# A hybrid decoder layer on one core: four adaLN chunks weighted on VectorE, low halves and three products on GpSimd, and a new order of issue up to the fourth FFN slice

## The chip, the core and the metric

The kernel runs on one NeuronCore of a Trainium2 chip. The metric is the device time of one execution in microseconds (us). Five engines take part: TensorE (PE, its weight loads are shown apart as PEld), VectorE (DVE), ScalarE (ACT), GpSimd (POOL) and SyncE (SP), whose queue issues nearly all transfers. A difference of 0.2% is about what a measurement of this kernel can tell from no change; the prediction says where it uses that.

## The reference, cut to what matters

One decoder layer over 256 tokens of width 1024, in float32:

```python
mod = (c @ w_ada[l] + b_ada[l])[:, None, :]
sh1, sc1, g1, sh2, sc2, g2 = jnp.split(mod, N_MOD, axis=-1)
h = rmsnorm(x, norm1_g[l]) * (1.0 + sc1) + sh1
z = h @ w_in[l]                       # q | k | v | x-branch | gate-branch, 512 columns each
attn = moba_attention(rmsnorm(q), rmsnorm(k), v)      # 256 keys: one block, causal
xr = causal_dwconv(xr, lru_conv_w[l], lru_conv_b[l])
lru = rg_lru(xr, ...) * jax.nn.gelu(gr)
mix = jnp.concatenate([rmsnorm(lru, lru_out_g[l]), rmsnorm(attn, attn_out_g[l])], axis=-1)
x = x + g1 * (mix @ w_out[l])
h2 = rmsnorm(x, norm2_g[l]) * (1.0 + sc2) + sh2
up = causal_dwconv(h2 @ w_up[l], ffn_conv_w[l], ffn_conv_b[l])
gate, val = jnp.split(up, 2, axis=-1)
x = x + g2 * ((jax.nn.silu(gate) * val) @ w_down[l])
```

Inside `rg_lru`: r and i are sigmoids of two block-diagonal products, a = exp(-8 r softplus(-lambda)), u = sqrt(1 - a*a) * (i * x), and h(t) = a(t) h(t-1) + u(t).

## The kernel before, in words

Activations lie with the width on the partitions: 8 blocks (kt = 0 to 7) of 128 rows by 256 tokens. Weights stream from HBM once, 1 MB at a time, into a ring of six buffers `w`; the list `order` fixes the order of the loads, and `send` issues the next one when `used` has counted the last reader of a buffer. A 2048-column buffer is read in two parts of 1024 columns.

Each large product runs as three one-pass products of float32r halves: `hi` casts a part of `w` to its high half `wh` (ACT, or DVE where its last argument is 1), `lo` subtracts it to leave the low half `wl` (line 172), and the activations are split the same way (`h_hi`, `h_lo`, `mix_h`, `mix_l`, `gated_h`, `gated_l`). All matmuls are issued on line 65. The stages are:

- lin: q, k, x-branch and gate-branch (`lin(kt, out, i)`, i is which of the three products). Beside it DVE makes shift and scale of norm 1 per block from the `ada1` loads (`ada`, line 365), and `normed`, `h_hi`, `h_lo`.
- the LRU: `conv_a`, `conv_d` (line 423), `gate`, `sigm`, `decay_a`, `decay_t`, `root` (ACT), `one_more` (line 452), the three products `igx` (439), `recur_u` (455), `recur_g` (462), and the scans (458).
- attention: sums and inverse roots for q and k (`k_sum`, `qk_r`), then for each of 8 heads `s_max` (DVE), `s_exp` (ACT, line 670), transposes `p_T` (676), copies `p_copy`, and `pv`. The matmuls of v fill in.
- `wo(c, kt)`, the output projection, and `res`, which adds it to x times g1; then norm 2 (`res_sq`, `res_add`, `res_sum`, `norm_s`, `norm_r`, `norm_mm`).
- 22 FFN slices: `up(f, kt)`, `gated_*`, `down(f, m)`.

The vectors g1 (load chunks 2 to 5) and sc2 (chunks 6 to 9) are sums over the 1024 entries of c; `g1_mm` runs each chunk as 8 float32 matmuls in four row groups of TensorE, with c as weights (`ccol`), `g1_row` copies four chunks to SBUF, and `g1_col` turns them to columns.

Up to the middle of slice 3 the order on all engines is one hand-held list of calls; from there a loop issues the slices. Each engine runs its instructions in the order of that list, and waits where an input is not there yet. GpSimd has only constants to set up before the first weights arrive.

Of the kernel before, what the change touches and what calls it, by code (L numbers as in the profile page):

```python
# [13 lines left out]
P = 128  # L14
# [54 lines left out]
def hybrid_layer(ctx: ExitStack, tc: tile.TileContext, x_d, c_d, pk_d, bd_d, ada1_d, lin_d, v_d,  # L69
# [47 lines left out]
    def send(q=None):  # L117

        if len(sent) < len(order):
# [3 lines left out]
            uses[key] = {"g1": 2 if key[1] < 2 else 1, "ada1": 2, "s2": 2, "g2": 2}.get(key[0], 4)  # L123
# [314 lines left out]
    def igx():  # L438
        nc.vector.tensor_mul(lru("ig"), lru("ig"), lru("xc"))
# [14 lines left out]
    def recur_u():  # L454
        nc.vector.tensor_mul(lru("ig"), lru("ig"), lru("r"))
# [5 lines left out]
    def recur_g():  # L461
        nc.vector.tensor_mul(lru("gel"), lru("gel"), lru("xc"))
# [162 lines left out]
    def g1_row(g, e=0):  # L625
        T["row", g] = pp.tile([P, 256], F32, tag="row", name="row")
        affine(e, T["row", g], B["g1", g].t[:, 0:256])

    def g1_col(g):
        b = B["g1", g]  # L630
        b.reopen(2)
        for m in range(2):
            b.mm(b.t[:, 256 + 4 * m:260 + 4 * m], T["row", g][:, m * P:(m + 1) * P], sel4)

    def g1_add(g):
        s = B["g1", g].t[:, 256:264].rearrange("p (m j) -> p j m", m=2)
# [102 lines left out]
    def res_add(kt):  # L739
        nc.vector.tensor_add(T["s2", kt], T["s2", kt], T["s2", kt - 1])  # L740
# [142 lines left out]
    sp(6)
    lin(1, "q", 1)
    normed(0, 2)
    lin(1, "g", 0)
    lin(1, "q", 2)
    lin(1, "x", 0)
    h_hi(0, 2)
    lin(1, "g", 2)  # L890
    lin(2, "q", 0)
    lin(2, "k", 0)
    lo("lin", 2, 0)
    hi("lin", 3, 0)
    lo("lin", 2, 1)
    lin(2, "k", 2)
    lin(2, "x", 2)
    hi("lin", 3, 1)
    ada("ada1", 1, 0)
    lin(2, "x", 0)  # L900
    ada("ada1", 1, 1)
    lin(2, "q", 2)
    lin(2, "g", 2)
# [84 lines left out]
    table(AF.Exp)
    lin(6, "g", 0)
    ada("ada1", 5, 1)  # L990
    table(AF.Gelu_apprx_tanh)
    ada_add("ada1", 5)
    sp(11)
    normed(0, 7)
    lin(5, "k", 2)
    hi("lin", 7, 0)
    lin(6, "q", 0)
    sp(12)
    lin(6, "x", 0)
    lin(4, "q", 1)  # L1000
    lin(6, "q", 1)
    h_hi(0, 7, 1)
    lin(6, "g", 2)
    sp(13)
    hi("lin", 7, 1)
    lin(6, "g", 1)
    h_lo(0, 7)
    lin(6, "x", 2)
    lin(6, "k", 0)
    bd_copy(1)  # L1010
    lo("lin", 7, 0)
    lo("lin", 6, 1)
    lin(6, "x", 1)
    lin(7, "x", 1)
    lin(7, "x", 2)
    lin(7, "x", 0)
# [60 lines left out]
    sigm(0, 3)
    v(0, 0, 0)
    qk_r(6)
    g1_mm(2)  # L1080
    sp(17)
    qk_r(7)
    lo("v", 1, 0)
    qk_r(8)
    sp(16)
    sigm(0, 1)
    qk_r(9)
# [472 lines left out]
```

## Time and profile before

| | |
|---|---|
| median of 3 runs | 332.96 us (332.39 to 333.06) |
| the profiled execution | 332.59 us |
| its span, first to last instruction | 330.8 us |
| TensorE busy | 320.2 us, 97% of the span |
| VectorE busy | 263.0 us, 79% |
| ScalarE busy | 194.5 us, 59% |
| GpSimd busy | 4.6 us, 1% |
| granted TensorE clock, mean | 0.991 |

Shares are means over stages with different limits, and a matmul counts as busy until its modelled end, so TensorE's 97% does not say that it has no room. Weight-load time (PEld) and the number of matmuls in a stretch tell more.

### The profile page before, as it was taken

How to read it: one execution, taken by the hardware profiler on the slowest of the kernel's cores; microseconds unless marked ns; L12 is line 12 of the kernel's file. 1: busy time of each engine (PE TensorE's matmuls, PEld its weight loads, DVE VectorE, ACT ScalarE, POOL GpSimd, SP SyncE). 2: the span in 40 equal slices, each digit the busy share in tenths (PEclk: the TensorE clock that was granted, in tenths of full speed). 3: DMA queues.
4: the chain of work that ended last, by engine and by line, in shares of the span. 5: the costliest groups of instructions: out<-in, count | busy, mean ns of one | idle time of the engine just before them, and what ended most of it. 6: DMA issues, size and time to landing. Idle time of an engine off the chain costs nothing.

```text
span 330.8 us, 6467 instructions
## 1 busy us (share of the span) xinstructions
PE 320.2 (97%) x2608; PEld 302.6 (91%) x2608; DVE 263.0 (79%) x507; ACT 194.5 (59%) x328; POOL 4.6 (1%) x22
## 2 busy tenths in 40 slices
PE   7899999999999999899999999999999999999994
PEld 7789999767599996899999999999999999999994
DVE  2469999899999998968696788888888677685654
ACT  5635458999988245865566455464646464655520
POOL 5000000000000000000000000000000000000000
PEclk9999999999999999799999999999999999999998
DMA  7999999939355998836566557575849463300003
GB/s 224 337 405 408 410 408 422 411 136 385 131 162 206 345 407 316 348 129 254 167 223 248 174 214 264 206 293 183 323 146 364 135 242 133 129 0 2 3 0 127
DMA packets 18013, 77.89 MB, mean 235 GB/s; under 512 B 1600, under 2 KB 6336, under 8 KB 10944
## 3 DMA queue, kind: packets, MB, share of 16 engines
q1 hardware_dynamic: 17840, 77.34, 62.6%
q8 instruction: 20, 0.33, 0.4%
q10 hardware_dynamic: 144, 0.15, 0.2%
q14 instruction: 9, 0.07, 0.1%
HBM read 76.43 MB, written 1.05 MB: 234 GB/s over the span
## 4 chain that ended last, share of the span: by engine, by line
PE 69%; DVE 16%; ACT 6%; issue 3%; SPq 2%; DMA 2%; DVEq 0%; ACTq 0%
PE bank L65 68%; DVE wl L172 4%; DVE w L365 4%; DMA w<-in_dram 2%; DVE m L423 2%; ACT wh L144 1%; SPq L132 1%; DVE m L766 1%; PE bank L676 1%; DVE ht L381 1%; ACT p L670 1%; DVE m L794 1%; DVE m L458 1%; DVE wh L150 1%; SPq L181 1%
## 5 line engine op out<-in xcount | busy, mean ns | idle before, releaser
L172 DVE TENSOR_TENSOR wl<-w,wh 128x1024 fp32r<-128x1024 f32 x94 | 113.2, 1220 | 19.8 <-ACT wh L144 19.1
L144 ACT CAST wh<-w 128x1024 fp32r<-128x1024 f32 x90 | 92.1, 1043 | 43.6 <-PE bank L65 34.9
L65 PE MATMUL bank<-hh__1575,wh 128*128 128x256 f32 x352 | 71.6, 285 | 1.1 <-ACT hh__1575 L148 1.1
L65 PE MATMUL bank<-hl__1576,wh 128*128 128x256 f32 x352 | 71.7, 286 | 0.0
L65 PE MATMUL bank<-hh__1575,wl 128*128 128x256 f32 x352 | 71.6, 285 | 0.0
L65 PEld LDWEIGHTS bank<-hh__1575,wh 128*128 128x128 f32 x352 | 55.3, 193 | 1.3 <-ACT hh__1575 L148 1.3
L65 PEld LDWEIGHTS bank<-hl__1576,wh 128*128 128x128 f32 x352 | 55.6, 194 | 0.2 <-DVE hl__1576 L392 0.2
L65 PEld LDWEIGHTS bank<-hh__1575,wl 128*128 128x128 f32 x352 | 55.4, 194 | 0.2 <-DVE wl L172 0.2
L766 DVE SCALAR_TENSOR_TENSOR m<-bank,pk,m 128x255 f32<-128x255 f32 x88 | 40.4, 479 | 19.0 <-ACT m L758 17.4
L65 PE MATMUL bank<-pl,wh 128*128 128x256 f32 x176 | 49.9, 284 | 0.4 <-DVE pl L782 0.4
L65 PE MATMUL bank<-ph,wh 128*128 128x256 f32 x176 | 49.9, 284 | 0.0
L65 PE MATMUL bank<-ph,wl 128*128 128x256 f32 x176 | 49.8, 283 | 0.0
L65 PEld LDWEIGHTS bank<-pl,wh 128*128 128x128 f32 x176 | 33.8, 192 | 0.6 <-DVE pl L782 0.6
L65 PEld LDWEIGHTS bank<-ph,wh 128*128 128x128 f32 x176 | 33.8, 192 | 0.1
L65 PEld LDWEIGHTS bank<-ph,wl 128*128 128x128 f32 x176 | 33.8, 192 | 0.0
L758 ACT ACTIVATE m<-bank,pk 128x256 f32<-128x256 f32 x44 | 22.4, 558 | 18.9 <-PE bank L65 18.9
L365 DVE CUSTOM_DVE_ANT_0 w<-w,cb 128x1024 f32<-128x1024 f32 x22 | 26.3, 1218 | 0.0
L770 ACT ACTIVATE m<-m 128x256 f32<-128x256 f32 x22 | 9.2, 417 | 26.8 <-DVE m L766 26.8
L65 PE MATMUL bank<-hl_mix__1178,wh 128*128 128x256 f32 x64 | 18.3, 286 | 0.2 <-DVE hl_mix__1178 L505 0.2
L65 PE MATMUL bank<-hh_mix__1177,wh 128*128 128x256 f32 x64 | 18.4, 288 | 0.0
L65 PE MATMUL bank<-hh_mix__1177,wl 128*128 128x256 f32 x64 | 18.1, 283 | 0.0
L65 PE MATMUL bank<-hh__245,wh 128*128 128x256 f32 x96 | 14.8, 283 | 1.0 <-DVE lt L345 1.0
(176 smaller groups left out, 429.5 us busy)
## 6 DMA issues: line engine op xcount, KB each, us to landing
w<-in_dram SPq DMA_DIRECT2D x55, 1024.0 KB, 5.1
w<-in_dram SPq DMA_DIRECT2D x32, 512.0 KB, 10.1
xT<-in_dram SPq DMA_DIRECT2D x4, 256.0 KB, 4.5
cb<-in_dram SPq DMA_DIRECT2D x1, 512.0 KB, 9.7
out_dram<-m SPq DMA_DIRECT2D x4, 128.0 KB, 2.5
out_dram<-m SPq DMA_DIRECT2D x2, 256.0 KB, 2.8
m<-in_dram SPq DMA_DIRECT2D x1, 256.0 KB, 9.5
pk<-in_dram ACTq DMA_DIRECT2D x1, 145.0 KB, 4.0
```

The source lines that it names most:

```text
L65: self.nc.tensor.matmul(out, lhsT, rhs, start=left == self.n, stop=left == 1, skip_group_check=True)
L132: (q or nc.sync).dma_start(raw[key][:, c:c + n], srcs[key[0]][key[1]][:, c:c + n])
L144: nc.scalar.copy(out, in_)
L150: nc.vector.tensor_copy(out, in_)
L172: (nc.vector if e else nc.gpsimd).tensor_sub(l[:, c], raw[key][:, c], h.bitcast(F32)[:, c])
L181: nc.sync.dma_start(xT[:, 2 * i:2 * i + 2, :], x_d[:, 2 * i:2 * i + 2, :])
L365: nc.vector.tensor_tensor_reduce(v[:, a, :], v[:, a, :], cb, scale=scale, scalar=0.0, op0=ALU.mult, op1=ALU.add, accum_out=mod[:, j, kt:kt ...
L381: nc.vector.scalar_tensor_tensor(T["ht", n, kt], xT[:, kt, :], mod[:, (SC1, SC2)[n], kt:kt + 1], rep, op0=ALU.mult, op1=ALU.mult)
L423: nc.vector.scalar_tensor_tensor(xc[:, t, s:], pair(B["x", t // 2])[:, t % 2, :S - s], col(O_CW + 4 * j + t), xc[:, t, s:], op0=ALU.mult, ...
L758: nc.scalar.activation(cv[:, s, :], pair(B["up", f])[:, s, :], AF.Identity, scale=col(O_FW + 88 + i), bias=col(O_FB + i))
L766: nc.vector.scalar_tensor_tensor(cv[:, s, d:], pair(B["up", f])[:, s, :S - d], col(O_FW + 44 * j + i), cv[:, s, d:], op0=ALU.mult, op1=ALU ...
L770: nc.scalar.activation(T["cv", f][:, 2, :], T["cv", f][:, 0, :], AF.Silu)
```

## The change

Four things change, all ahead of the loop over slices.

1. `g1`'s chunks 2 to 5: instead of 8 matmuls each, DVE multiplies the eight 256-column pieces of a chunk by their entry of c and adds them up (`g1_acc`, 8 instructions a chunk, 32 in all); TensorE only sums the result over the partitions (`ga_col`, two matmuls a chunk). One `g1_row` and one `g1_col` go. A chunk's buffer `w` is free after the eighth `g1_acc`.
2. 32 of the low halves (`lo` with a last argument of 0) run on GpSimd: 10 of the 16 of lin, all 4 of v, all 8 of wo, and 10 of the first 12 of up and down weights. So do the five additions of norm 2 (`res_add`) and the three products `igx`, `recur_u`, `recur_g`.
3. 13 more casts `hi` run on DVE (17, before 4), and some smaller copies and high halves move from ACT to DVE.
4. The list of calls up to slice 3 is in another order; from slice 4 on it is the same.

```diff
-            uses[key] = {"g1": 2 if key[1] < 2 else 1, "ada1": 2, "s2": 2, "g2": 2}.get(key[0], 4)
+            uses[key] = {"g1": 2 if key[1] < 2 else 8 if key[1] < 6 else 1, "ada1": 2, "s2": 2, "g2": 2}.get(key[0], 4)
...
-    def igx():
-        nc.vector.tensor_mul(lru("ig"), lru("ig"), lru("xc"))
+    def igx(e=1):
+        (nc.vector if e else nc.gpsimd).tensor_mul(lru("ig"), lru("ig"), lru("xc"))
...
+    def recur_u(e=1):
+        (nc.vector if e else nc.gpsimd).tensor_mul(lru("ig"), lru("ig"), lru("r"))
...
+    def recur_g(e=1):
+        (nc.vector if e else nc.gpsimd).tensor_mul(lru("gel"), lru("gel"), lru("xc"))
...
+    def g1_acc(i, kt):
+
+        w = raw["g1", i].rearrange("p (k n) -> p k n", k=KT)[:, kt, :]
+        c = col(O_C + kt)
+        if kt == 0:
+            T["ga", i] = pp.tile([P, 256], F32, tag="ga", name="ga")
+            nc.vector.tensor_scalar(T["ga", i], w, c, None, op0=ALU.mult)
+        else:
+            nc.vector.scalar_tensor_tensor(T["ga", i], w, c, T["ga", i], op0=ALU.mult, op1=ALU.add)
+        used(("g1", i))
+
+    def ga_col(i):
+        j = i - 2
+        b = get(B, "ga", lambda: bank(0, 8))
+        for m in range(2):
+            o = 4 * j + 2 * m
+            b.mm(b.t[:, o:o + 2], T["ga", i][:, m * P:(m + 1) * P], ones[:, 0:2])
+
+    def ga_add():
+        nc.vector.tensor_add(mod[:, G1, :], B["ga"].t[:, 0:16:2], bada[:, G1, :])
...
-    def res_add(kt):
-        nc.vector.tensor_add(T["s2", kt], T["s2", kt], T["s2", kt - 1])
+    def res_add(kt, e=1):
+        (nc.vector if e else nc.gpsimd).tensor_add(T["s2", kt], T["s2", kt], T["s2", kt - 1])
...
-    recur_u()
+    recur_u(0)
...
+    lo("v", 0, 0, 0)
```

Three places show how the instructions move. The first is DVE between the sums of squares of q and k and the normed k; before, low halves and casts of v and wo (`wl`, `wh`) stand between the small steps of the inverse roots (`tqk`, `iqk`):

```order
L172 TENSOR_TENSOR wl<-w,wh 128x1024
L259 TENSOR_SCALAR iqk<-mqk 128x32
L150 CAST wh<-w 128x1024
L261 TENSOR_TENSOR tqk<-iqk,mqk 128x32
L150 CAST wh<-w 128x1024
L263 TENSOR_TENSOR tqk<-tqk,iqk 128x32
L355 SCALAR_TENSOR_TENSOR lt<-lt 128x4
L265 SCALAR_TENSOR_TENSOR iqk<-tqk,iqk 128x32
L150 CAST wh<-w 128x1024
```

and of the change, at the same place (`ga` is the sum that `g1_acc` builds, `pk` holds c):

```order
L259 TENSOR_SCALAR iqk<-mqk 128x32
L620 TENSOR_SCALAR ga<-w,pk 128x256
L261 TENSOR_TENSOR tqk<-iqk,mqk 128x32
L622 SCALAR_TENSOR_TENSOR ga<-w,pk,ga 128x256
L263 TENSOR_TENSOR tqk<-tqk,iqk 128x32
L622 SCALAR_TENSOR_TENSOR ga<-w,pk,ga 128x256
L265 SCALAR_TENSOR_TENSOR iqk<-tqk,iqk 128x32
```

The 1024-column subtractions and casts have gone from between the steps, and 256-column steps of g1 stand there.

The second place is DVE after the root of the recurrence, up to the second head's maximum. Before (`bank` to `p` with `mask` is `s_max`):

```order
L452 SCALAR_TENSOR_TENSOR m_828<-m_885,m_828 128x1024
L455 TENSOR_TENSOR m_819<-m_819,m_828 128x1024
L458 SCALAR_TENSOR_TENSOR m_743<-m_885,m_819 128x256 x4
L661 ISA p,mn<-bank_971,mask 128x128
L661 ISA mn 128x1
L663 ISA p,mn<-bank_971,mask 128x256
L663 ISA mn 128x1
L665 SCALAR_TENSOR_TENSOR eb<-mn,iqk 128x2
```

and of the change (line numbers of `s_max` are 679 to 683 there):

```order
L452 SCALAR_TENSOR_TENSOR m_874<-m_896,m_874 128x1024
L622 SCALAR_TENSOR_TENSOR ga<-w,pk,ga 128x256
L679 ISA p,mn<-bank_955,mask 128x128
L679 ISA mn 128x1
L681 ISA p,mn<-bank_955,mask 128x256
L681 ISA mn 128x1
L683 SCALAR_TENSOR_TENSOR eb<-mn,iqk 128x2
L622 SCALAR_TENSOR_TENSOR ga<-w,pk,ga 128x256 x2
```

The first head's maximum no longer stands behind the product `recur_u` (455) and the four scans (458); a second one follows, and the scans come after it.

The third place is GpSimd's queue behind its constants. Before, it ends there:

```order
L205 MEMSET sel 64x1
L206 MEMSET sel 64x1
L212 COPY sel_127<-ident 32x4 x4
L214 MEMSET bd 128x1024
L244 COPY ccol<-pk 128x8 x3
```

and of the change, from the same `bd` on:

```order
L214 MEMSET bd 128x1024
L172 TENSOR_TENSOR wl<-w,wh 128x1024 x5
L244 COPY ccol<-pk 128x8
L172 TENSOR_TENSOR wl<-w,wh 128x1024 x6
L244 COPY ccol<-pk 128x8
L172 TENSOR_TENSOR wl<-w,wh 128x1024 x2
L244 COPY ccol<-pk 128x8
L172 TENSOR_TENSOR wl<-w,wh 128x1024
L439 TENSOR_TENSOR m_847<-m_847,m_733 128x1024
L455 TENSOR_TENSOR m_847<-m_847,m_874 128x1024
L462 TENSOR_TENSOR m_792<-m_792,m_733 128x1024
L172 TENSOR_TENSOR wl<-w,wh 128x1024 x8
```

The eight low halves of wo stand behind the three products. Five additions of 128x256 and ten more low halves of up and down weights follow.

## Rows read from the trace of the kernel before

**Rows 1.** The page's busy time of each engine, share of the span, instructions.

```profile
PE 320.2 (97%) x2608; PEld 302.6 (91%) x2608; DVE 263.0 (79%) x507; ACT 194.5 (59%) x328; POOL 4.6 (1%) x22
```

**Rows 2.** Stretches: length; busy PE, PEld, DVE, ACT, POOL; granted clock; DMA share, GB/s.

```profile
20.00:58.00 38.00, 37.66 (x280) 34.94 (x273) 36.82 (x72) 22.07 (x28) 0.00 (x0) 1.00 1.03 412
58.00:78.00 20.00, 19.50 (x131) 15.01 (x130) 18.67 (x41) 19.04 (x36) 0.00 (x0) 1.00 0.73 297
78.00:88.00 10.00, 9.74 (x67) 6.38 (x65) 9.51 (x29) 9.26 (x20) 0.00 (x0) 1.00 0.72 283
88.00:100.00 12.00, 11.99 (x110) 10.11 (x109) 11.44 (x43) 11.03 (x37) 0.00 (x0) 1.00 0.43 139
100.00:126.00 26.00, 25.82 (x222) 24.80 (x221) 23.34 (x48) 13.62 (x25) 0.00 (x0) 1.00 0.82 323
126.00:133.00 7.00, 5.54 (x70) 3.67 (x68) 6.31 (x17) 3.72 (x8) 0.00 (x0) 1.00 0.78 302
155.00:331.00 176.00, 171.33 (x1427) 171.03 (x1425) 132.14 (x207) 90.16 (x138) 0.00 (x0) 0.99 0.48 171
```

**Rows 3.** The chain that ended last, 58 to 108 us: start, length, work.

```profile
58.77 1.48 ACT m L148 x3
...
78.18 1.24 DVE m L452
...
79.44 1.24 DVE m L455
...
80.77 1.99 DVE m L458 x4
...
83.97 2.24 ACT p L670 x8
...
99.53 8.13 PE bank L65 x66
```

**Rows 4.** Groups by line and shape: count, busy us, mean ns, idle before.

```profile
L172 DVE TENSOR_TENSOR wl<-w,wh 128x1024 fp32r<-128x1024 f32 x94 | 113.2, 1220 | 19.8 <-ACT wh L144 19.1
...
L392 DVE SCALAR_TENSOR_TENSOR hl__1576<-ht,mod,hh__1575 128x256 fp32r<-128x256 f32 x8 | 3.7, 480 | 0.3 <-ACT hh__1575 L148 0.2
...
L150 DVE CAST wh<-w 128x1024 fp32r<-128x1024 f32 x4 | 2.7, 687 | 0.0
...
L152 DVE TENSOR_SCALAR hh__245<-ht,mod 128x256 fp32r<-128x256 f32 x3 | 1.1, 354 | 0.0
```

**Rows 5.** TensorE's instructions in order of time: start us, length us.

```profile
69.34 1.07 PE L65 MATMUL bank<-w,ccol 128*32 128x256 f32 x16
...
88.90 0.61 PE L65 MATMUL bank<-ones,m 128*128 128x2 f32 x4
...
97.23 0.51 PE L65 MATMUL bank<-sel,row 128*128 128x4 f32 x4
```

**Rows 6.** ScalarE's instructions between the root and the first exponential.

```profile
78.05 1.04 ACT L144 CAST wh<-w 128x1024 fp32r<-128x1024 f32 x1
79.00 0.57 ACT L144 COPY m<-bank 128x512 f32<-128x512 f32 x1
...
81.95 1.28 ACT L670 ACT_TABLE_LOAD   x1
```

**Rows 7.** Groups of GpSimd by line and shape, as in rows 4.

```profile
L209 POOL MEMSET ccol<- 128x1024 f32 x1 | 1.0, 951 | 0.0
...
L197 POOL TENSOR_SCALAR_AFFINE_SELECT ident<-ident 128x128 f32<-128x128 f32 x1 | 0.3, 292 | 0.0
```

**Rows 8.** The chain that ended last, at norm 2.

```profile
126.68 0.42 ACT sr L737
127.10 0.63 ACT wh L144
...
127.95 0.42 ACT sr L737
```

**Rows 9.** A stretch at the first FFN slice, columns as in rows 2.

```profile
135.00:136.00 1.00, 1.00 (x6) 1.00 (x6) 1.00 (x4) 0.72 (x3) 0.00 (x0) 0.50 1.01 426
```

**Rows 10.** Waits of SP's queue: us in total, times, longest.

```profile
SPq L132 <- DVE wl L172: 153.6, 35, 8.8
```

More of the change, by code (lines that the diff above doesn't have):

```diff
@@ L888, in hybrid_layer @@
[L888 to L891, printed above, removed]
+    h_lo(0, 2)
+    ada("ada1", 1, 0)
+    ada("ada1", 1, 1)
+    lin(2, "g", 0)
+    hi("lin", 3, 0)
+    ada_add("ada1", 1)
+    normed(0, 3)
+    table(AF.Gelu_apprx_tanh)
+    sp(9)
+    sp(10)
+    lin(2, "q", 1)
+    lin(2, "g", 1)
+    h_hi(0, 3, 1)
+    lin(1, "k", 0)
+    h_lo(0, 3)
+    hi("lin", 3, 1)
+    lin(1, "k", 1)
+    table(AF.Exp)
+    sp(11)
+    lin(2, "g", 2)
+    lin(2, "x", 1)
+    lo("lin", 2, 1, 0)
@@ new lines, in hybrid_layer @@
+    ada_add("ada1", 2)
+    normed(0, 4)
+    lin(3, "g", 2)
+    lin(3, "q", 0)
+    table(AF.Gelu_apprx_tanh)
+    lin(3, "x", 0)
+    lin(3, "x", 2)
+    lin(1, "q", 2)
+    lin(2, "x", 0)
+    lin(2, "q", 0)
+    hi("lin", 4, 0, 1)
+    h_hi(0, 4)
+    sp(14)
+    lo("lin", 3, 1)
+    lin(3, "g", 1)
+    lin(3, "q", 1)
+    lo("lin", 4, 0, 0)
+    hi("lin", 4, 1)
+    lin(3, "k", 0)
+    lin(4, "g", 0)
+    h_lo(0, 4)
+    lin(4, "k", 0)
+    lin(3, "k", 1)
+    ada("ada1", 3, 0)
+    sp(13)
@@ L991, in hybrid_layer @@
[L991 to L1000, printed above, removed]
[L1001 to L1016 removed]
+    lin(5, "g", 2)
@@ new lines, in hybrid_layer @@
+    lin(5, "k", 1)
+    hi("lin", 7, 0)
+    sp(16)
+    normed(0, 6)
+    h_hi(0, 6, 1)
+    ada("ada1", 5, 0)
+    lo("lin", 6, 0, 0)
+    h_lo(0, 6)
+    lin(5, "g", 1)
+    lin(5, "q", 2)
+    ada("ada1", 5, 1)
+    ada_add("ada1", 5)
+    lin(6, "x", 0)
+    lin(5, "x", 0)
+    hi("lin", 7, 1)
+    lin(6, "k", 0)
+    normed(0, 7)
+    lin(6, "g", 0)
+    h_hi(0, 7, 1)
+    lin(6, "q", 0)
+    lin(5, "k", 2)
+    lin(6, "x", 2)
+    lin(6, "x", 1)
+    lin(5, "g", 0)
+    h_lo(0, 7)
+    lo("lin", 7, 0)
@@ L1077, in hybrid_layer @@
+    qk_r(5)
+    qk_r(6)
+    sigm(1, 3)
+    v(1, 1, 0)
+    g1_acc(3, 3)
+    table(AF.Sigmoid)
+    sigm(0, 1)
+    c_more(2)
+    qk_r(7)
+    g1_acc(3, 4)
+    sigm(1, 0)
+    lo("v", 1, 1, 0)
+    sigm(0, 0)
+    qk_r(8)
+    g1_acc(3, 5)
+    qk_r(9)
+    sigm(0, 2)
+    g1_acc(2, 3)
     sigm(0, 3)
     v(0, 0, 0)
[L1079 to L1087, printed above, removed]
+    qk_r(10)
+    sigm(1, 1)
     decay_a(0)
+    g1_acc(3, 6)
@@ L1118, in hybrid_layer @@
[L1118 to L1132 removed]
+    ga_col(3)
+    k_n(1)
+    k_n(0)
+    decay_t(1)
+    v(1, 2, 0)
+    g1_acc(4, 0)
+    k_T(0)
+    v(1, 0, 0)
+    k_T(1)
+    v(0, 2, 0)
+    decay_t(3)
+    g1_acc(2, 4)
+    g1_acc(4, 1)
+    v(0, 2, 1)
+    decay_t(2)
+    g1_acc(2, 5)
+    root()
+    k_copy(0)
@@ L1133, in hybrid_layer @@
+    g1_acc(4, 2)
+    g1_acc(4, 3)
+    g1_acc(2, 6)
+    k_copy(1)
+    g1_acc(4, 4)
+    one_more()
+    sc(0)
+    g1_acc(4, 5)
+    v(1, 0, 1)
+    igx(0)
+    s_max(0)
+    recur_u(0)
+    v_copy(0)
+    g1_acc(2, 7)
+    g1_acc(4, 6)
+    v(0, 1, 1)
+    s_exp(0)
+    hi("wo", 1, 1)
+    v(1, 1, 1)
+    s_max(1)
+    recur_scan(3)
+    s_exp(1)
+    hi("wo", 0, 0)
+    recur_scan(2)
+    recur_scan(0)
+    v(1, 2, 1)
+    p_T(0)
+    p_copy(0, 0)
+    recur_scan(1)
+    g1_acc(4, 7)
     sc(1)
-    s_exp(0)
@@ new lines, in hybrid_layer @@
+    mix_h(7)
+    mix_l(7)
+    wo(2, 2)
+    wo(0, 4)
+    mix_h(6)
+    mix_l(6)
+    table(AF.Sqrt)
+    g1_acc(5, 7)
+    ada("s2", 0, 0)
+    mix_h(5, 1)
+    mix_l(5)
+    wo(0, 6)
+    wo(2, 4)
+    wo(2, 7)
+    wo(0, 5)
+    ada("s2", 1, 1)
+    wo(2, 6)
+    ada("s2", 1, 0)
+    wo(1, 6)
+    wo(2, 5)
+    ada("s2", 3, 1)
+    ga_col(5)
+    hi("wo", 3, 0, 1)
+    ada("s2", 2, 0)
+    hi("wo", 3, 1)
+    ada_add("s2", 0)
+    wo(1, 4)
+    ada("s2", 3, 0)
+    lo("wo", 3, 0, 0)
+    wo(0, 0)
```

822 lines of the change are left out of this document (360 added, 462 removed).

## The prediction

> **What bounds the kernel now.** I read the busy times first: TensorE is busy 97% of the span, DVE 79%, GpSimd 1% [rows 1]. A busy TensorE need not be a full one, so the stretches come next [rows 2]. From 155 us to the end 1427 matmuls take 171.3 us, 0.120 us each, and weight loads fill 171.0 us: this is a full TensorE, and the change touches none of it. From 20 to 58 us (lin) TensorE is full too, 37.7 of 38.0 us; its weight loads, 34.9 us, are fewer because some matmuls are 512 columns wide. DVE is equally full there, 36.8 us, and the loads run at 412 GB/s, so three resources share this bound and relieving one buys nothing. From 58 to 100 us TensorE has room: weight loads fill 15.0 of 20, 6.4 of 10, 10.1 of 12 us, and DVE (39.6 of 42) and ACT (39.3 of 42) are full. From 100 to 126 us it is full again, and at norm 2 (126 to 133 us) it has room, 3.7 of 7 us. So at most 5.0 + 3.6 + 1.9 + 3.3 = 13.8 us is to be won in the stretches where TensorE has room, and much of that is not free, since the small float32 matmuls there load few weights.
>
> The chain of waits says who holds these stretches [rows 3]: from 58.8 us it runs through ACT's and DVE's steps of the recurrence (`one_more` 78.18, `recur_u` 79.44, the scans 80.77), reaches the first exponential at 83.97 us, and by 99.53 us it lies on TensorE alone. The sum below is made against the profiled execution, 332.59 us (330.8 of span, 1.8 around it), which is 0.4 us under the median of 332.96.
>
> **TensorE's work.** A g1 chunk takes 1.07 us of TensorE (16 records at 69.34), the four 4.3 us; `g1_col` takes 0.51 us; the new sums have the form of two matmuls against ones, 0.61 us a chunk (88.90), 2.4 us [rows 5]. The work falls by 4.3 + 0.5 - 2.4 = 2.4 us. Three of the removed chunks lie ahead of 84 us, where TensorE waits anyway, and three of the four new sums lie behind it: on the full part the balance is 1.07 + 0.51 - 3 x 0.61 = -0.25, a loss of 0.25 us. What is freed earlier helps only as far as v's matmuls move into it. Bounds: 0.25 us lost, 2.4 us gained; I take 1.0 gained.
>
> **DVE.** In lin 10 low halves of 1.22 us go, 6 casts of 0.69 and 3 high halves of 0.35 come [rows 4]: -12.2 + 4.1 + 1.1 = -7.0 us, 29.8 of 38. It buys nothing while TensorE and the loads stay full. From 58 to 100 us 8 low halves (9.8) and three products of the same shape (3.7) go, and about 25 steps of `g1_acc` come: 21 at the 0.48 us of the nearest three-operand row, 4 at 0.35, 11.5 us [rows 4]. With about 1 us of copies taken from ACT, DVE stands at about 38.6 us where it had 39.6: the g1 chunks eat what the low halves gave. What differs is the order. The 1024-column instructions between the steps of the inverse roots become 256-column ones, which is worth little: the chain leaves DVE for ACT soon after.
>
> **The first exponential.** Before, ACT runs cast, copy, cast, copy, cast, table load behind the root, at 78.05, 79.00 and on to the load at 81.95 [rows 6], and then waits for DVE, where the first head's maximum stands behind `one_more` 1.24, `recur_u` 1.24 and four scans 1.99 us [rows 3]. In the change the maximum stands behind `one_more` and one `g1_acc`, and ACT has three copies and the table load ahead of it: 78.05 + 3 x 0.57 + 1.28 = 81.0 us where it was 83.97, 3.0 us earlier. Two of the casts, 1.04 us each, are now issued between the exponentials, so 2.1 us of the 3.0 come back later on ACT; on the other side two of the heads' copies go to DVE. Bounds 0 and 3.0; I take 1.0, about what is left when the casts are paid.
>
> **Norm 2.** On the chain a cast of up-weights lies 0.63 us between the last two squares on ACT (127.10, with a square at 126.68 and one at 127.95) [rows 8]. In the change two of these casts are on DVE, and neither stands between them. Bounds 0 and 0.63; I take 0.6. Behind it TensorE runs at half clock, 1.2 of 2.4 GHz, granted 0.50 from 135 to 136 us [rows 9], after the stretch to 133 us with its waits [rows 2]. I count nothing for it, though a shorter gap might keep the clock.
>
> **GpSimd.** Its new work is 32 low halves, 3 products and 5 additions, and no row shows such an instruction. The nearest are a memset of the same 128x1024 shape, which reads nothing, 0.95 us, and a 128x128 select with one input, 0.29 us, eight of which make 2.34 us [rows 7]. I take 1.65, the middle; the rows lie equally far. At 1.65 ten low halves fill 16.5 of lin's 38 us, so as a queue GpSimd has time. Each low half also frees a load buffer: SP waits 153.6 us for DVE's low halves in all [rows 10], and for the moved ones it will wait for GpSimd. With six buffers I count nothing for 0.4 us (1.65 against 1.22) each. `recur_u` and `recur_g` are in series with the recurrence and lose 0.4 us each, but the exponentials no longer wait for them.
>
> The largest unknown is whether GpSimd's reads hold DVE up. Below, nothing; above, DVE and GpSimd take turns throughout. In none of the stretches does GpSimd do anything [rows 2]. What speaks for the lower bound is that DVE's low halves take 1.22 us in the mean [rows 4], while they run beside loads of 412 GB/s and an ACT that is full from 58 to 78 us [rows 2]: no other reader of the same memory is seen to stretch them. That is an argument from other engines, so I take nothing for the likeliest case and give the upper bound a large chance of its own.
>
> The Trainium skill, "SBUF — State Buffer", section "Who interferes with whom", speaks against the change: a DVE instruction with two inputs in SBUF contends with a GpSimd instruction that reads SBUF, and the one that starts first holds the shared ports until it ends. No row here shows it; by that rule the first rival below comes true. The skill's "GPSIMD Engine Reference", section "Performance versus the Vector engine", times a two-input add of 2048 columns at 4497 ns; half of it, 2.25 us as an estimate, lies inside my bounds, and lin's sum in that rival would be 29.8 + 22.5 = 52.3 us by it.
>
> **The sum.** 332.6 - 1.0 - 1.0 - 0.6 = 330.0 us. With all bounds: 332.6 - 2.4 - 3.0 - 0.6 = 326.6 and 332.6 + 0.25 = 332.9.
>
> **Rivals.**
> 1. DVE and GpSimd take turns. In lin nearly every DVE instruction reads two SBUF tiles; 29.8 + 10 x 1.65 = 46.3 us has to fit into 38, 8.3 more. From 58 to 84 us four low halves of v and two products, 6 x 1.65 = 9.9 us, meet a DVE with about 1.5 us free, 8.4 more. 332.6 - 2.6 + 16.7 = 346.7 us. At 0.95 us it is 1.3 + 4.2 more, 335.5; at 2.34 us 15.2 + 12.5 more, 357.7. Against it: pieces of DVE's work read PSUM, and GpSimd's work may fall into DVE's waits. It decides once the 35 long instructions hold DVE up by more than 2.6 us in all, 0.07 us each.
> 2. No turns, but GpSimd is slow and late: at 2.34 us `recur_u` and `recur_g` lose 1.1 us each on the way to the normed recurrence, and wo's eight low halves, queued behind `recur_g`, take 18.7 us, from about 87 to 106 us, when TensorE wants the first at 99.5 [rows 3]. With the loads set back by one low half (1.1 us): 332.6 - 2.6 + 2.2 + 1.1 = 333.3, up to 335.
> 3. Nothing is gained: TensorE's work that is taken away before 84 us was in its waits, and ACT pays the earlier start back in full: 332.6 + 0.25 - 0.6 = 332.3.
>
> **How the numbers follow.** Forecast 0.44, rival 1 0.33, rival 2 0.13, rival 3 0.10. The bound between faster, same and slower is 0.2%, 0.67 us about 332.96, what a measurement of this kernel can tell from no change. The forecast is faster; rival 1 is slower; of rival 2 0.10 is slower and 0.03 the same; of rival 3 0.08 is the same and 0.02 faster. So faster 0.46, same 0.11, slower 0.43. The forecast's own range is 326.6 to 332.9. For 8 in 10 the range goes from 326.5 to 346.5: it leaves out half of rival 1 (0.17) and the few cases below.
>
> **What would show it.** Right: DVE's 1024-column rows keep 1.22 us beside GpSimd's low halves; lin's matmuls stay full from 20 to 58 us; the first exponential starts near 81 us; the stretch of 7 us at norm 2 is shorter. Rival 1: the same DVE rows get longer or stand behind gaps while a GpSimd instruction runs, and weight loads in lin fall below 34.9 in 38 us. Rival 2: TensorE or the recurrence waits for `wl` or line 455 from GpSimd, with DVE's rows as they were. The prediction is wrong if DVE's busy time ahead of 155 us grows although 35 of its long instructions have left it.

## The result and the profile after

The changed kernel takes 384.72 us (median of 4 runs, 383.67 to 385.73), the kernel before, run beside it, 333.01 (332.39 to 333.29): a ratio of 1.1555, 95% interval 1.1512 to 1.1599. It is 51.7 us slower, where 2.96 us faster was forecast; the time lies outside the range. The profiled execution spans 382.1 us, 51.3 more than before.

First the page's busy times of each engine:

```profile
PE 335.9 (88%) x2556; PEld 315.6 (83%) x2556; DVE 305.0 (80%) x526; ACT 178.5 (47%) x301; POOL 100.0 (26%) x62
```

Against [rows 1] 35 long VectorE instructions have gone to GpSimd (42.7 us at 1.22), and the 32 steps of g1 and 13 casts that came make up 24.3 us at 0.48 and 0.69 us; yet VectorE is busy 42.0 us longer, 305.0 for 263.0. An engine that got less work and shows more busy time spends that time inside its instructions, waiting. The stretches of [rows 2], with one more for the steady part (columns as there):

```profile
20.00:58.00 38.00, 29.38 (x180) 26.49 (x181) 36.63 (x52) 11.56 (x14) 19.69 (x8) 0.89 0.97 364
58.00:78.00 20.00, 16.56 (x110) 15.51 (x110) 17.52 (x23) 4.93 (x8) 8.01 (x4) 0.87 0.66 245
78.00:88.00 10.00, 7.51 (x43) 5.35 (x42) 9.71 (x16) 8.30 (x15) 6.67 (x4) 0.95 0.17 54
88.00:100.00 12.00, 9.43 (x30) 6.82 (x28) 11.96 (x27) 6.34 (x14) 6.31 (x4) 0.61 0.42 168
100.00:126.00 26.00, 20.11 (x110) 15.64 (x110) 24.66 (x63) 17.06 (x39) 11.99 (x5) 0.78 0.44 161
...
206.00:382.00 176.00, 171.62 (x1415) 171.30 (x1415) 129.78 (x205) 87.19 (x133) 4.92 (x2) 0.99 0.46 168
```

In lin (20 to 58 us) weight loads fall from 34.9 to 26.5 us, and VectorE is full with 52 instructions where it did 72. The granted clock was 1.00 in all these stretches before; now it is 0.61 to 0.95, and TensorE is busy for less of them (29.4 us of lin's 38, where it was 37.7). The last row is the same 176 us of full TensorE as before: nothing is lost behind 206 us. Where VectorE's time goes is seen in the groups by line and shape (mean ns of one behind the busy time):

```profile
L172 POOL TENSOR_TENSOR wl<-w,wh 128x1024 fp32r<-128x1024 f32 x32 | 82.3, 2586 | 95.7 <-DVE wh L150 37.3 <-ACT wh L144 35.2 <-DVE lt L353 10.8
L172 DVE TENSOR_TENSOR wl<-w,wh 128x1024 fp32r<-128x1024 f32 x62 | 74.9, 1221 | 18.1 <-ACT wh L144 17.3
L150 DVE CAST wh<-w 128x1024 fp32r<-128x1024 f32 x17 | 18.3, 1087 | 4.2 <-DMA w<-in_dram 4.2
L622 DVE SCALAR_TENSOR_TENSOR ga<-w,pk,ga 128x256 f32<-128x256 f32 x28 | 18.2, 669 | 0.1
L381 DVE SCALAR_TENSOR_TENSOR ht<-xT,mod,rrep 128x256 f32<-128x256 f32 x7 | 7.7, 1101 | 0.2
```

A cast of line 150 takes 1087 ns in the mean where it took 687 [rows 4]; line 381 with the reciprocal norm in SBUF (`rrep`) grew from 483 to 1101 ns. These means mix two lengths: of the seven of line 381 five kept 0.48 us, and two, one inside a low half of GpSimd and one 0.03 us ahead of one, took 2.58 and 2.72. Steps with an operand in PSUM keep their time even there. Three of line 423, the second and third of which begin inside a low half of GpSimd, by the timeline:

```profile
84.17 1.50 DVE L423 SCALAR_TENSOR_TENSOR m<-bank,pk,m 128x255 f32<-128x255 f32 x3
84.26 5.09 POOL L172 TENSOR_TENSOR wl<-w,wh 128x1024 fp32r<-128x1024 f32 x2
```

Three of them take 1.51 us at 80.57 us, where GpSimd does nothing. Read one by one, 33 VectorE instructions of the changed kernel are over 0.15 us longer than their form is elsewhere, by 57 us in all, and each of the 33 begins inside a GpSimd instruction with two SBUF inputs (once 0.03 us ahead of it). What ran from start to end inside one reads PSUM, or is a sum over one tile or the read-out of such a sum.

The low halves that stayed on VectorE show nothing (1221 ns): they were the sign that the prediction told the reader to look at, and by them alone one would have missed it. None of the 62 begins while GpSimd runs a low half: 54 come behind GpSimd's last one, six more fall ahead of its first or into its pauses, and two (at 43.96 and 198.53 us) begin 0.2 us ahead of one.

The chain of waits at norm 2, and its last piece of TensorE:

```profile
168.69 2.33 DVE t L280
171.04 2.27 DVE t L281
173.34 2.27 DVE rms L282
175.66 1.24 PE bank L65 x4
...
205.91 170.12 PE bank L65 x1403
```

Three instructions on 128x2 elements, 0.16 us each before, take 2.3 us each, and TensorE waits for them. The timeline of GpSimd there shows three low halves of the up-weights without a gap, one beside each of the three:

```profile
168.65 6.93 POOL L172 TENSOR_TENSOR wl<-w,wh 128x1024 fp32r<-128x1024 f32 x3 [3.75 <-DVE rms L279]
```

The long last piece begins at 205.91 us, where the matmul that opens it stood at 154.69: 51.2 of the 51.3 us are lost ahead of it. Last, SP's queue (us in total, times, longest) waits 125.0 us for VectorE's low halves, fewer than in [rows 10], but another 86.2 for GpSimd's:

```profile
SPq L132 <- DVE wl L172: 125.0, 26, 9.9
SPq L132 <- POOL wl L172: 86.2, 15, 14.3
```

### The profile page after: what moved, and what is told of

Read it like the earlier page. It is cut to its first block, busy times and chain, and to the rows that moved or that the text cites. A ratio compares the mean times of both kernels' runs of the same rounds, so it can differ in the third digit from the quotient of the medians.

```text
span 382.1 us, 6416 instructions
## 1 busy us (share of the span) xinstructions
PE 335.9 (88%) x2556; PEld 315.6 (83%) x2556; DVE 305.0 (80%) x526; ACT 178.5 (47%) x301; POOL 100.0 (26%) x62
## 4 chain that ended last, share of the span: by engine, by line
PE 56%; DVE 32%; DMA 4%; SPq 3%; issue 3%; ACT 2%; DVEq 0%; ACTq 0%
PE bank L65 55%; DVE w L365 4%; DVE wh L150 4%; DMA w<-in_dram 4%; DVE ga L622 4%; DVE ht L381 2%; DVE hl__1583 L392 2%; DVE hh__249 L152 1%; DVE mod L375 1%; DVE m L423 1%; DVE eb L683 1%; SPq L132 1%; SPq L128 1%; SPq L185 1%; DVE hl_mix__1170 L505 1%
## 5 line engine op out<-in xcount | busy, mean ns | idle before, releaser
L172 POOL TENSOR_TENSOR wl<-w,wh 128x1024 fp32r<-128x1024 f32 x32 | 82.3, 2586 | 95.7 <-DVE wh L150 37.3
L144 ACT CAST wh<-w 128x1024 fp32r<-128x1024 f32 x77 | 79.0, 1042 | 54.6 <-PE bank L65 33.1
L172 DVE TENSOR_TENSOR wl<-w,wh 128x1024 fp32r<-128x1024 f32 x62 | 74.9, 1221 | 18.1 <-ACT wh L144 17.3
L65 PE MATMUL bank<-hl__1583,wh 128*128 128x256 f32 x352 | 71.8, 286 | 1.7 <-DVE hl__1583 L392 1.7
L65 PE MATMUL bank<-hh__1582,wh 128*128 128x256 f32 x352 | 72.0, 286 | 1.1 <-ACT hh__1582 L148 1.1
L65 PE MATMUL bank<-hh__1582,wl 128*128 128x256 f32 x352 | 71.7, 285 | 1.2 <-DVE wl L172 1.2
L65 PEld LDWEIGHTS bank<-hl__1583,wh 128*128 128x128 f32 x352 | 55.7, 195 | 1.9 <-DVE hl__1583 L392 1.9
L65 PEld LDWEIGHTS bank<-hh__1582,wh 128*128 128x128 f32 x352 | 55.8, 195 | 1.4 <-ACT hh__1582 L148 1.4
L65 PE MATMUL bank<-ph,wh 128*128 128x256 f32 x176 | 50.7, 288 | 1.6 <-ACT ph L144 1.6
L65 PE MATMUL bank<-ph,wl 128*128 128x256 f32 x176 | 50.6, 287 | 0.0
L65 PEld LDWEIGHTS bank<-ph,wh 128*128 128x128 f32 x176 | 34.6, 196 | 1.9 <-ACT ph L144 1.8
L150 DVE CAST wh<-w 128x1024 fp32r<-128x1024 f32 x17 | 18.3, 1087 | 4.2 <-DMA w<-in_dram 4.2
L65 PE MATMUL bank<-hh__249,wh 128*128 128x256 f32 x96 | 15.2, 294 | 6.8 <-DVE hh__249 L152 6.8
L65 PEld LDWEIGHTS bank<-hh__249,wh 128*128 128x128 f32 x96 | 13.6, 199 | 8.5 <-ACT warm L222 4.1
```

The source lines that it names most:

```text
L65: self.nc.tensor.matmul(out, lhsT, rhs, start=left == self.n, stop=left == 1, skip_group_check=True)
L144: nc.scalar.copy(out, in_)
L150: nc.vector.tensor_copy(out, in_)
L172: (nc.vector if e else nc.gpsimd).tensor_sub(l[:, c], raw[key][:, c], h.bitcast(F32)[:, c])
```

## The experiments

Two theories stood at the start. A, taking turns: GpSimd's instructions that read SBUF hold VectorE up, and it them. B, lateness: GpSimd's results come late, whatever VectorE does. A third one, C, was added with the first run: the rest of the change (g1 on VectorE, casts on VectorE, the order) overloads VectorE by itself. Differences below are of medians to the kernel before in the same group of runs, in us.

**1. Everything on VectorE** (the changed kernel, its GpSimd low halves, products and sums back on VectorE):

```diff
-        (nc.vector if e else nc.gpsimd).tensor_sub(l[:, c], ...)
+        nc.vector.tensor_sub(l[:, c], ...)
```

> The changed kernel in its own order, with every GpSimd instruction of the change (32 low halves, 3 products, 5 additions) on VectorE instead. Theory A, VectorE waits for GpSimd's reads: the 52 us that were lost go with GpSimd; VectorE gets 45 us of its own work back, some of it on the path, so 333 to 345 us. Theory B, the new order and the late low halves cost the time, whichever engine makes them: it stays over 370 us. Theory C, the g1 chunks and the casts overload VectorE: about 360 us or more, since VectorE is then the fullest engine ahead of slice 4.

It took 368.04 us (366.88 to 368.85), ratio 1.109 (1.1037 to 1.1142), +36.0. This is nearest to C. So taking GpSimd away doesn't bring the time of before back. The run isn't a clean price of the order, though: steps that were written for two queues now stand in one, in order.

**2. Only lin's ten low halves on GpSimd** (the kernel before):

```diff
-        (nc.vector if e else nc.gpsimd).tensor_sub(l[:, c], ...)
+        (nc.gpsimd if (kind, i, part) in ON_POOL else nc.vector).tensor_sub(l[:, c], ...)
```

> The kernel before in its own order, with 10 of lin's 16 low halves (the same ten as in the change) on GpSimd. Theory A: in lin VectorE's 36.8 us less 10 x 1.22 plus 10 x 2.4 that it has to wait are 48.6 us where 38 are, so about 343 us (338 to 346). Theory B, GpSimd is only late: the low halves end 1.2 us later each, which the buffers partly hide, 333 to 336 us. Theory C, order and g1: 333 us, no change.

It took 346.91 us, ratio 1.0465 (1.0423 to 1.0506), +14.9, just above A's range: 1.49 us for each of ten instructions that left a full engine. The groups and the stretch of lin (as above):

```profile
L173 POOL TENSOR_TENSOR wl<-w,wh 128x1024 fp32r<-128x1024 f32 x10 | 29.5, 2963 | 34.5 <-ACT wh L145 34.5
```
```profile
20.00:58.00 38.00, 31.05 (x219) 28.29 (x208) 35.67 (x45) 14.60 (x18) 22.52 (x9) 0.96 0.95 366
```

VectorE has ten instructions less to do and is nearly as full as before, with 45 instructions instead of 72. Here one of its own low halves does begin inside one of GpSimd's (39.43 to 42.93 us), and it takes 3.41 us instead of 1.22:

```profile
40.60 3.41 DVE L173 TENSOR_TENSOR wl<-w,wh 128x1024 fp32r<-128x1024 f32 x1
```

Nothing else was changed, so A holds in lin.

**3. GpSimd as long, but hardly reading** (the changed kernel; each of the 32 low halves becomes a subtraction of one column and three memsets, meant to take 2.4 us and taking 2.9; these low halves are zero but for that column):

```diff
+            nc.gpsimd.tensor_sub(l[:, d], raw[key][:, d], h.bitcast(F32)[:, d])
+            for z in (slice(1, 1024), slice(1, 1024), slice(1, 513)):
+                nc.gpsimd.memset(...)
```

> The changed kernel with each low half of GpSimd replaced by a one-column subtraction, which keeps the waits, and three memsets of the low half's tile, about 2.4 us in all, so GpSimd is as long busy but reads nothing; the low halves themselves are left out. Products and additions stay on GpSimd. Theory A, if reads are what VectorE waits for: most of the 52 us is gone, 335 to 350 us. If writes hold VectorE as well: 375 to 385. Theory B, the low halves come late: 375 to 385 us too, but with VectorE's rows at their lengths of before.

It took 347.26 us (two runs), ratio 1.0466 (1.0391 to 1.054), +15.3. Queue, order and all else are those of the changed kernel, GpSimd is busy even longer, and 36.4 of the 51.7 us are gone. This is what it costs that these 32 instructions read, 1.14 us each. The busy times say the same:

```profile
PE 324.1 (94%) x2556; PEld 307.9 (89%) x2556; DVE 262.0 (76%) x526; ACT 178.2 (52%) x301; POOL 105.1 (31%) x158
```

The same 526 VectorE instructions take 262.0 us here and 305.0 in the changed kernel: 43.0 us of waiting that was booked as work. The three instructions at norm 2 take 0.16 us each here. Not every turn is gone, though: 25 instructions are still held, by 17 us in all, beside the products on GpSimd and beside the one-column subtractions and memsets; nine of them are casts:

```profile
L150 DVE CAST wh<-w 128x1024 fp32r<-128x1024 f32 x17 | 16.4, 977 | 2.8 <-DMA w<-in_dram 2.5 <-PE bank L65 0.3
```

So lateness alone (B) is at most the +15.3, if the parts add up.

**4. The dispute measured by itself.** The layer is left out; six VectorE instructions of one kind run alone, and then beside four GpSimd instructions.

> A kernel that leaves the layer out and runs forms of VectorE alone and beside GpSimd subtractions, memsets and copies of 128x1024. Theory A: a GpSimd subtraction takes about 2.35 us alone; beside it a VectorE 128x2 subtraction of two SBUF tiles goes from 0.16 us to about 2.4 us, a 128x1024 one waits a whole GpSimd instruction now and then, instructions that read one SBUF tile or PSUM keep their time, and casts are stretched as in the changed kernel (0.69 to 1.09 us in the mean). Theory B: all VectorE forms keep their times.

The timeline, in pairs: alone, then beside GpSimd, whose row stands behind it (start, us for all of them):

```profile
23.82 9.23 POOL L90 TENSOR_TENSOR po<-pa,pb 128x1024 f32<-128x1024 f32 x4
...
34.59 6.89 DVE L99 TENSOR_TENSOR do<-da,db 128x1024 f32<-128x1024 f32 x6
43.32 15.37 DVE L99 TENSOR_TENSOR do<-da,db 128x1024 f32<-128x1024 f32 x6
43.17 12.18 POOL L90 TENSOR_TENSOR po<-pa,pb 128x1024 f32<-128x1024 f32 x4
...
61.01 0.50 DVE L102 TENSOR_TENSOR do<-da,db 128x2 f32<-128x2 f32 x6
63.41 6.87 DVE L102 TENSOR_TENSOR do<-da,db 128x2 f32<-128x2 f32 x6
...
74.49 3.69 DVE L105 CAST dr<-da 128x1024 fp32r<-128x1024 f32 x6
80.03 12.17 DVE L105 CAST dr<-da 128x1024 fp32r<-128x1024 f32 x6
...
94.26 3.67 DVE L108 TENSOR_TENSOR do<-bank,db 128x512 f32<-128x512 f32 x6
99.76 3.67 DVE L108 TENSOR_TENSOR do<-bank,db 128x512 f32<-128x512 f32 x6
99.61 9.25 POOL L90 TENSOR_TENSOR po<-pa,pb 128x1024 f32<-128x1024 f32 x4
...
128.81 9.90 DVE L114 TENSOR_SCALAR do<-da,db 128x256 f32<-128x256 f32 x6
...
162.07 6.89 DVE L99 TENSOR_TENSOR do<-da,db 128x1024 f32<-128x1024 f32 x6
161.90 3.63 POOL L93 MEMSET po<- 128x1024 f32 x4
171.02 7.00 DVE L105 CAST dr<-da 128x1024 fp32r<-128x1024 f32 x6
170.84 3.63 POOL L93 MEMSET po<- 128x1024 f32 x4
```

Six subtractions take 6.89 us alone and 15.37 beside GpSimd, whose four take 12.18 for 9.23: each waits for the other's whole instruction. Six instructions on two columns go from 0.50 to 6.87 us, since three of them wait for a GpSimd instruction each; six casts go from 3.69 to 12.17, and six products of a 128x256 tile with a scalar per partition (line 114) from 1.66 to 9.90, although the expectation had instructions that read one tile keep their time. Beside four GpSimd copies, which read one tile each, six subtractions take 10.14 us. With one operand in PSUM nothing changes on either side (3.67 and 3.67, 9.25 for 9.23). Memsets leave the subtractions alone (6.89) and hold a cast (3.69 to 7.00). The Trainium skill, "SBUF — State Buffer", section "Who interferes with whom", states this: two SBUF inputs against a reading GpSimd instruction, the whole instruction long, and casts in a two-port mode against any. The trace agrees in each of these pairs.

**5. Only g1 on VectorE** (the kernel before, one `g1_acc` behind each of the steps that follow the old places):

```diff
-    g1_mm(3)
+    g1_acc(3, 0)
     qk_r(2)
+    g1_acc(3, 1)
     ...
```

> The kernel before with one part of the change alone: g1's chunks 2 to 5 are multiplied by c and accumulated on VectorE (8 instructions each, spread over the steps that follow the old place), and TensorE only sums them over partitions. All low halves and products stay on VectorE. 32 instructions of about 0.48 us (the probe's two-input 128x256 form) are 15 us of VectorE between 68 and 100 us, where it was busy 38.6 of 42 us already. If VectorE bounds that stretch, 10 to 15 us come on top: 343 to 348 us. If TensorE's relief there carries more than VectorE's load, 329 to 333 us.

It took 354.73 us, ratio 1.0675 (1.0623 to 1.0727), +22.0, more than expected. (VectorE was busy 39.6 of 42 us from 58 to 100 us; the 38.6 is the prediction's sum for the change.) The chain of waits runs through VectorE from 66.9 to 82.6 us without a gap, and the new instructions stand in it, at the 0.48 us that the prediction took (the chain counts 0.4 of it, the rest overlaps the next):

```profile
70.24 0.42 DVE ga L622
70.66 0.60 DVE wh L150
```
```profile
100.00:126.00 26.00, 22.26 (x106) 21.32 (x107) 17.68 (x58) 12.95 (x34) 0.00 (x0) 0.54 0.33 121
```

The first exponential comes at 92.1 us, 8.1 late. From 78 to 100 us TensorE gets 82 matmuls where it had 177, and from 100 to 126 us its granted clock is 0.54 in the mean, near the lower of its levels (1.2 of 2.4 GHz): 106 matmuls where there were 222. What goes beyond the expected 15 us falls between the exponential and wo, which starts 21.9 us late.

**6. The best case of the rest** (the changed kernel; each of the 32 low halves is one column and one memset, meant to take 1.0 us and taking 1.2, and is left at zero but for that column; products and sums on VectorE):

```diff
+        if e == 0:
+            c = slice(part * 1024, part * 1024 + 1)
         (nc.vector if e else nc.gpsimd).tensor_sub(l[:, c], ...)
+        if e == 0:
+            nc.gpsimd.memset(l.bitcast(F32)[:, part * 1024 + 1:part * 1024 + 1024], 0.0)
```

> The changed kernel with its 32 GpSimd low halves made into a one-column subtraction and one memset (about 1.0 us, no read of SBUF to speak of; the low halves are thus left at zero), and the three products and the sums of squares back on VectorE. It is the most that the new order and the g1 part can give where GpSimd's reads cost nothing. If the reads are the whole loss: 322 to 331 us, under the kernel before. If the new order or the g1 products lose time by themselves: 338 us or more, and the difference to the run with memsets of 2.4 us (347.3) is what their length, the products and the sums cost.

It took 338.79 us (336.48 to 341.14), ratio 1.0196 (1.0116 to 1.0276), +6.1. So even with 32 low halves taken off VectorE cheaply, the change loses. It isn't a clean price of the order and g1, since turns are left here too: 11 VectorE instructions are held by 6 us in all, six of them casts (687 ns before):

```profile
L150 DVE CAST wh<-w 128x1024 fp32r<-128x1024 f32 x17 | 14.7, 873 | 2.9 <-DMA w<-in_dram 2.3 <-PE bank L65 0.5
```

The stretch ahead of wo and the chain there, in the profiled execution, the longest of the four (341.14):

```profile
88.00:100.00 12.00, 10.21 (x55) 8.59 (x54) 9.98 (x38) 9.35 (x27) 3.18 (x6) 0.62 0.75 262
```
```profile
97.32 0.64 PE bank L698 x3
...
102.20 0.64 PE bank L698 x3
...
108.35 0.34 PE bank L698 x3
```

The first exponential starts at 85.5 us, 1.5 later than before, not 3.0 earlier. The granted clock is 0.62 from 88 to 100 us, where it was 1.00. Three transposes of a head take 0.64 us in most of this piece and 0.34 at its end; before they took 0.33 to 0.55. The attention gets longer, and wo starts at 110.0 us for 100.2.

**7. The order and the casts on VectorE** (run 1 with g1 back on TensorE; chunks 3 and 2 stand behind the last gate that needs their bank):

```diff
-    g1_acc(3, 0)
-    ...
+    g1_mm(3)
```

> The changed kernel's order with everything of GpSimd on VectorE, as in the run that gave 368.0 us, and g1's chunks 2 to 5 back on TensorE. What is left of the change is its order. If the g1 products on VectorE made those 368.0 us so long, 32 x 0.48 us come off: 351 to 356 us. If the order did it (casts that stand on VectorE in it, low halves late), 362 to 368 us. An order that is harmless by itself would give 331 to 336 us.

It took 358.69 us, ratio 1.081 (1.0749 to 1.0872), +26.0, between the two expectations: g1 on VectorE is 10.0 of run 1's 36.0, and the order and the 13 more casts, on one queue, are the rest. As in run 1, that is an order made for two queues.

**8. The prediction's second term by itself** (the kernel before; k's copies ahead of wo's casts, the first two heads ahead of the scans):

```diff
+    k_copy(1)
     hi("wo", 0, 1)
     recur_u()
+    sc(0)
+    s_max(1)
+    s_max(0)
     ...
+    s_exp(1)
     recur_scan(1)
```

> The kernel before with the first pair of heads ahead of the recurrence: both copies of k's transposes stand ahead of the casts of wo, and the scores, the two maxima and the first two exponentials ahead of the four scans; all work is the same. The first exponential should start near 81.3 us in place of 83.97. If it sets the end, as the prediction took it for a term of 1.0: 1.0 to 2.7 us less, 330 to 332 us. If another chain sets it (VectorE's load from 84 to 126 us, or the casts of wo that now come later): 332.5 to 335 us.

It took 333.1 us (10 runs) to 332.74, ratio 1.0011 (0.9985 to 1.0037). ScalarE's timeline and TensorE's at wo's first matmul:

```profile
81.47 0.50 ACT L670 ACTIVATE p<-p,eb,iqk 128x128 f32<-128x128 f32 x1
...
99.86 0.37 PE L65 MATMUL bank<-hh_mix__1177,wh 128*128 128x256 f32 x1
```

The first exponential is 2.5 us earlier, wo 0.3, the end nothing. The first exponential doesn't set the end. What does is in the chain of waits, behind the two maxima:

```profile
82.09 2.36 DVE m L458 x4
84.47 1.24 DVE m L462
```

The scans, which stood ahead of the exponential, now stand behind it, and what follows waits for them: the transposes of the next head begin at 87.20 us, where they began at 87.63, and from there to wo the chain lies on TensorE in both, 12.7 and 12.6 us.

**9 and 10. One low half beside steps that read PSUM** (v's first, on GpSimd beside the convolution; in 10 together with the edit of 8):

```diff
     conv_d(0)
+    lo("v", 0, 0, 0)
 ...
-    lo("v", 0, 0)
```

> The kernel before with one low half (v's first) on GpSimd, put behind the convolution's first step: from about 61.7 to 64.1 us, where VectorE reads PSUM only (60.28 to 66.07), and taken out of VectorE's chain without gaps at 67.37. The probe's PSUM-reading forms kept their times beside GpSimd. If turns are taken only over SBUF reads: the convolution's twelve rows keep 0.48 us, VectorE's chain from 66 us comes 1.1 us earlier, and the end 0 to 1.1 us: 331.6 to 332.7 us. If GpSimd holds VectorE whatever it reads: the convolution is 1 to 2.3 us later, 333 to 335 us.

> The same low half on GpSimd, together with the order in which the first two heads stand ahead of the scans. With the first exponential near 80.2 us in place of 83.97. If VectorE's sum of work from 66 to 100 us sets the start of wo, as the run with the early exponential alone suggests (exponential 2.5 us earlier, end the same): as with the low half alone, 331.6 to 332.7 us. If both gains add: 330 to 331.5 us.

They took 332.3 us, ratio 0.9988 (0.9967 to 1.0009), and 332.54, ratio 0.9994 (0.9968 to 1.002), of 12 runs each: neither can be told from no change. The timelines of 9:

```profile
60.33 5.79 DVE L423 SCALAR_TENSOR_TENSOR m<-bank,pk,m 128x255 f32<-128x255 f32 x12 [0.55 <-ACT m L148]
61.78 2.41 POOL L172 TENSOR_TENSOR wl<-w,wh 128x1024 fp32r<-128x1024 f32 x1 [56.37 <-ACT wh L144]
```

The twelve steps take 5.79 us, as long as without GpSimd: A's limit holds in the kernel too, and VectorE is 1.0 us ahead behind it. It buys nothing there: in 9 the chain goes through ScalarE and TensorE to ScalarE's table load, which starts at 71.09 us, 71.17 before. In 10 the chain lies on TensorE from 66.3 to 77.7 us and then runs over the scans at 82.05 us, as in run 8.

**11. Only the products and sums on GpSimd** (the kernel before, `igx`, `recur_u`, `recur_g` and `res_add` with `nc.gpsimd`):

> The kernel before with only the change's products on GpSimd: the three of the recurrence and the sums of squares of norm 2; all low halves on VectorE, g1 on TensorE. Two of the three products stand on the chain of waits (1.23 us each before, 2.45 us as GpSimd rows in the changed kernel), and the sums wait for each other. If their length counts: 2 x 1.2 us and some turns of about 2.3 us in VectorE's chain, 335 to 340 us. If VectorE's relief (7 x 0.4 to 1.2 us) pays for it: 331 to 333.5 us.

It took 338.67 us, ratio 1.0193 (1.016 to 1.0227), +5.8. The chain of waits:

```profile
70.72 2.29 DVE tqk L261
...
81.55 2.39 POOL m L455
...
86.97 1.87 DVE eb L665
```

`recur_u` takes 2.39 us in the chain where it took 1.24; a step of 0.10 us (line 261) and one of 0.17 (line 665) each wait for most of a product.

The landmarks in us, read from the profiled execution of each (9 and 10 lie within 0.1 us of before and of 8 up to wo):

| kernel | lin's last matmul | first exponential | wo | end |
|---|---|---|---|---|
| before | 63.0 | 84.0 | 100.2 | 330.8 |
| changed | 79.9 | 107.7 | 134.0 | 382.1 |
| 1 all on VectorE | 73.8 | 99.6 | 124.5 | 366.1 |
| 2 lin's low halves | 78.9 | 99.2 | 115.4 | 344.6 |
| 3 memsets of 2.9 us | 64.2 | 88.7 | 109.9 | 344.0 |
| 5 g1 alone | 62.8 | 92.1 | 122.1 | 352.6 |
| 6 memset of 1.2 us | 63.8 | 85.5 | 110.0 | 339.3 |
| 7 order and casts | 71.7 | 93.8 | 117.4 | 356.8 |
| 8 early exponential | 62.5 | 81.5 | 99.9 | 331.3 |
| 11 products alone | 62.8 | 88.9 | 106.7 | 336.4 |

## Why the prediction was wrong

**The step that failed** is in the part on GpSimd: "no other reader of the same memory is seen to stretch them. That is an argument from other engines, so I take nothing for the likeliest case". That VectorE keeps its time beside ScalarE and the transfers says nothing about GpSimd. The probe and runs 2 and 3 put turns in place of the nothing: 36.4 of the 51.7 us for the reads of the low halves. The first rival had the mechanism, and got 0.33; the profile held no row that spoke against it.

**The rival's price was too small as well.** It gave 346.7 us, at most 357.7. With 1.65 us for a GpSimd instruction it had 8.3 us for lin and 16.7 for all up to 84 us; with the 2.34 us that was measured, 15.2 and 27.7. Lin's last matmul came 16.9 us late and the first exponential 23.7, so up to there the sum is good with the right price. What it missed is behind that: wo starts 33.8 us late and the last long piece of TensorE 51.2. The rival left out the low halves of wo and of the up-weights, and at norm 2, where VectorE's chain is three instructions of 0.16 us, each waits 2.1 us. It also left out the clock: the mean granted clock went from 0.991 to 0.931. How much of the 51.7 us that is can't be separated by these runs, since much of the slow time falls where TensorE waits anyway.

**GpSimd's price**, 1.65 us as the middle of 0.95 and 2.34, measured 2.34 us alone and 2.59 in the kernel. That the eight selects make the same 2.34 is luck: a GpSimd copy of 128x1024, which reads one tile, took 1.04 us in the probe, so no row of before had the price of two inputs. The second rival's other half, late results, isn't shown by itself: it is part of the 9.2 us between runs 3 and 6, with what the longer memsets hold and with the products, which cost 5.8 alone in run 11.

**TensorE's work** (1.0 gained) and **VectorE's sum** ("the g1 chunks eat what the low halves gave"): the price of an instruction was right, 483 ns in run 5 for 480. But the sum counted the low halves' time as gone from VectorE, and it came back as waiting. Put on VectorE without that relief, g1 alone costs 22.0 us (run 5). With the relief, and 6 us of turns left, g1, the casts and the order together lose 6.1 (run 6), where the prediction had 2.6 gained: the first exponential came 1.5 us late, and wo, behind a stretch granted 0.62 of the clock, 9.8.

**The first exponential** (1.0 gained): its time was forecast well for an order like this one, 81.0 us for 81.47 in run 8; that it is worth anything was wrong. The chain of waits names the instruction that came last, but the scans that were put behind the exponential took its place at once.

**Norm 2** (0.6 gained) lost 6.4 us, three waits of 2.1 beyond the 0.16. Where the low halves hardly read (run 3) these three keep 0.16. What the moved casts gained there can't be read beside that.

**What would show it**: VectorE's busy time did grow, as the last sentence said of a wrong prediction: 175.2 us ahead of 206 us, where it was 130.8 ahead of 155. The other sign, the mean of VectorE's low halves, failed: they kept 1221 ns in the changed kernel, because none of them began inside a GpSimd instruction. Held is what stands next in VectorE's queue, and in run 2 that was a low half once (3.41 us).

**Where the 51.7 us went**, then: 36.4 to turns over the low halves' reads (changed kernel to run 3); 9.2 to the length of GpSimd's work and to the products and sums, turns of theirs among them (run 3 to 6); 6.1 to the order, g1 and the casts on VectorE, with the turns that memsets still cause (run 6 to before). By the intervals of the runs each of these is known to 3 or 4 us. What of the last is the order and what is g1 and the casts stays open, for in runs 1, 5 and 7 VectorE carries low halves that it doesn't have in the change. No version here beats the kernel before.

## What to carry to other kernels

GpSimd is no free engine beside a VectorE that works from SBUF: each of its reading instructions held the VectorE instruction that began inside it, however short, until its own end, up to 2.3 us, if that one had two operands in SBUF or was a cast or a product with a scalar per partition. Beside steps that read PSUM it held nothing (run 9), though there it also bought nothing. An unknown that no row of the profile shows isn't nothing: where other engines are the only witness, take the bound that a mechanism gives, or probe it; and an engine that loses work and gains busy time is waiting inside its instructions, and the single instructions show it where a mean can hide it.

## What the runs showed of the hardware that was not expected

- The wait doesn't scale with the VectorE instruction: 128x2 elements go from 0.15 to 2.3 us, 128x1024 from 1.22 to 3.3.
- GpSimd pays as well where VectorE's instruction is long: its subtraction takes 3.05 us in the mean (12.18 for four) beside VectorE's subtractions, 2.31 (9.23) beside those of two columns.
- Beside memsets, which read nothing, a cast is held through all four, 3.63 us in a row (the first cast takes 4.00 us, six casts 7.00 for 3.69), where beside subtractions the two engines alternate.
